# Matmul stages of a decoder layer: one work pool of aligned tiles, weights combined ahead of the resident rows, and shared in the attention output

## The chip, the cores and the metric

The kernel runs on one core of a Trainium2 chip. The metric is the device time of one execution in microseconds (us); lower is better. The engines of the core are TensorE (PE, matmuls), VectorE (DVE), ScalarE (ACT), GpSimd (POOL) and SyncE (SP, which here issues the DMA transfers). Each works through its own instructions in order and waits for others by semaphores.

## The reference

One layer with two parallel branches, on x of 2048 x 1024 in float32:

```python
shift, scale, gate = split(silu(c) @ w_ada + b_ada, 3)
h = x * (1 + scale) + shift
q, k, v, g_attn, u, b_gate, c_gate, g_conv, m_attn, m_conv = split(h @ w_in)
# o: three dilated causal sliding-window attention groups, merged by their softmax sums
a_out = (o * silu(g_attn)) @ w_attn_out
z = c_gate * u                          # zp: z behind two zero rows
y_conv = cw[0] * zp[:-2] + cw[1] * zp[1:-1] + cw[2] * zp[2:] + conv_b
s_out = (b_gate * y_conv * silu(g_conv)) @ w_conv_out
merged = sigmoid(m_attn) * a_out + sigmoid(m_conv) * s_out
y = merged @ w_o
out = layer_norm(2 ** 0.25 * x + (1 + gate) * y) * ln_g + ln_b
```

## The kernel before

Each float32 operand is split into a high and a low part, and a product is three matmuls (high x high, high x low, low x high; lines L681 to L683). Part 1, up to about 1202 us, makes scale and shift, the attention's projections, the attention and its merge; the merge's last work on DVE runs on to 1239 us. The change doesn't touch it.

The last stage (from L596 on) computes all other products as Strassen-Winograd products of 2 x 2 blocks, seven instead of eight. Two kinds of operands go into these:

- T, the resident side: `t_row` makes, from two wide tiles (`big`) with one row of blocks each, the seven combinations of row i, split into th and tl (11 operations on DVE, the rest on ACT). Four rows of T stay on the chip for a whole stage.
- S, the streamed weights: `stationary_parts` loads two blocks (`raw`), forms the combinations (`xs`, `s4`, in place in `raw`) and splits them into w2h, w2l, w1h and w1l (eight operations on DVE). Each step has its own S.

A step's `products` are 7 products x 4 rows x 3 = 84 matmuls of 128x512, in the order 1, 2, 6, 5, 7, 4, 3. ACT copies three intermediate sums out of PSUM (`t` tiles, L687), and a consumer takes the results on DVE. `step` loads and forms S, runs the products of the step before (`flush`) and puts its own on the list `todo`; so S is one step ahead of its products. At the start of a stage `flush` comes first, then T's rows, and then the first step's S.

The stages in order, each but the second with a pool of its own (`workspace(number of big, number of t)`):

1. Projections and their consumers, pool (4, 8): for p = 0, 1 (halves of the sequence) four rows of T and 24 steps (conv and gates alternating, then eight mixes). p = 1 starts within the same pool.
2. Attention output, pool (7, 8): for p = 0, 1 two rows of T (of om_scr) and four steps of half size (S of 128x512), each with two big tiles of sigmoid values loaded from sg_scr and stored to pa_scr. During p = 0 `gate_part` makes the gate from w_ada on DVE (L236).
3. Conv output, pool (6, 8): for p = 0, 1 four rows of T (of y_scr) and four steps; each loads two tiles of sg_scr and two of pa_scr, POOL adds the two (L890), and mg_scr is stored.
4. w_o and layer norm ("norm stage"), pool (5, 6): the rows of T are those of w_o, times the gate (L916); then eight steps with S made of mg_scr, and the norm on DVE, ACT and POOL (L927 to L944), two result tiles a step.

The order of the work on each engine is set when the program is built: a scheduler orders what the code writes by estimated times; tiles of a pool are used in turn, and a new use waits until the old one is done.

Of the kernel before, what the change touches and what calls it, by code (L numbers as in the profile page):

```python
# [11 lines left out]
F32 = mybir.dt.float32  # L12
F32R = mybir.dt.float32r
AF = mybir.ActivationFunctionType
# [40 lines left out]
def layer_kernel(ctx: ExitStack, tc: tile.TileContext, x, xm, xn, cvec, wada, bada, w_main, w_v,  # L55
# [548 lines left out]
    def big():  # L604
        return work[0].tile([P, PAIR + 2], F32, name="big", bufs=work[1])

    def half(name="t"):
        return work[0].tile([P, CH], F32, name="t", bufs=work[2])

    @contextmanager  # L610
    def workspace(n_big, n_half):
        with tc.tile_pool(name="work", bufs=1, reuse_waits="tile") as w:
            work[:] = [w, n_big, n_half]
            yield w
# [30 lines left out]
    def stationary_parts(w, raw1, raw2, n):  # L645
# [21 lines left out]
        s4 = w.tile([P, n], F32, name="s4")  # L667
# [47 lines left out]
    def step(w, src1, src2, n, T, rows, consumer):  # L715
        raws = []
        for s in ((src1, src2) if src2 is not None else (src1,)):
            raw = w.tile([P, DM], F32, name="raw", bufs=3)
            SP.dma_start(raw, s)
# [13 lines left out]
    gate_acc = const.tile([P, 4], F32, name="gate_acc")  # L733

    with workspace(4, 8) as w:
        for n in range(KT):
            SP.dma_start(cw[:, n, :3], convw[n])
        SP.dma_start(cw[:, :, 3], convb)
        for p in range(2):
            T = {}  # L740
            flush()
            for i in range(4):
                xa, xb = big(), big()
                for t, k in ((xa, i), (xb, i + 4)):
                    for cc in range(2):
                        SP.dma_start(t[:, cc * CH:(cc + 1) * CH], xn[2 * p + cc, :, k, :])
                    S.activation(t[:, :PAIR], t[:, :PAIR], AF.Identity, scale=scp[:, k:k + 1],
                                 bias=mod[:, 0, k:k + 1])
                t_row(T, i, xa, xb)
            for n in range(KT):  # L750
                box = {}

                def conv(box=box, n=n):
                    z = box["z"] = big()
                    V.tensor_copy(z[:, 0:2], halo[:, n, :])

                    def zmul(at):
                        def f(r, bank):
                            t = half()
                            V.tensor_add(t, r, bank)  # L760
                            V.tensor_mul(z[:, 2 + at:2 + at + CH], t, z[:, 2 + at:2 + at + CH])
                        return f

                    def u1(r, bank):
                        V.tensor_add(z[:, 2 + CH:], r, bank)
                        V.tensor_mul(z[:, 2 + CH:], z[:, 2 + CH:], box["c1"])
                        V.tensor_copy(halo[:, n, :], z[:, PAIR:])
                        y = box["y"] = big()[:, :PAIR]
                        S.activation(y, z[:, 0:PAIR], AF.Identity, scale=cw[:, n, 0:1], bias=cw[:, n, 3:4])
                        V.scalar_tensor_tensor(y, z[:, 1:PAIR + 1], cw[:, n, 1:2], y, op0=ALU.mult, op1=ALU.add)  # L770
                        V.scalar_tensor_tensor(y, z[:, 2:PAIR + 2], cw[:, n, 2:3], y, op0=ALU.mult, op1=ALU.add)

                    def c1(r, bank):
                        box["c1"] = half()
                        V.tensor_add(box["c1"], r, bank)

                    return sum_to(z[:, 2:2 + CH]), u1, zmul(0), c1

                def gates(box=box, n=n, p=p):
                    g = big()[:, :PAIR]  # L780
                    y = box["y"]

                    def g1(r, bank):
                        V.tensor_add(g[:, CH:], r, bank)
                        V.tensor_mul(y, y, g)
                        S.activation(g, g, AF.Sigmoid)
                        V.tensor_mul(y, y, g)
                        V.tensor_mul(y, y, box["b"])
                        SP.dma_start(y_scr[p, n], y)

                    def bs(at):
                        def f(r, bank):
                            V.tensor_add(box["b"][:, at:at + CH], r, bank)
                        return f

                    box["b"] = big()[:, :PAIR]
                    return sum_to(g[:, :CH]), g1, bs(0), bs(CH)

                step(w, w_main[W_U + n], w_main[W_C + n], CH, T, range(4), conv)
                step(w, w_main[W_GC + n], w_main[W_B + n], CH, T, range(4), gates)  # L800
            for d in range(KT):
                def mixes(p=p, d=d):
                    m = [big()[:, :PAIR] for _ in range(2)]

                    def out_(k):
                        S.activation(m[k], m[k], AF.Sigmoid)
                        SP.dma_start(sg_scr[p, k, d], m[k])

                    def c12(r, bank):
                        V.tensor_add(m[0][:, CH:], r, bank)  # L810
                        out_(0)

                    def c21(r, bank):
                        V.tensor_add(m[1][:, :CH], r, bank)
                        out_(1)

                    return sum_to(m[0][:, :CH]), c12, c21, sum_to(m[1][:, CH:])

                step(w, w_main[W_MA + d], w_main[W_MC + d], CH, T, range(4), mixes)
        flush()  # L820


    with workspace(7, 8) as w:
        cbox = []

        def gate_part(k):
            if k == 0:
                cbox.append(w.tile([P, DM], F32, name="cb"))
                silu_c(cbox[0], big()[:, :DM])
            wt = w.tile([P, DM], F32, name="raw", bufs=3)  # L830
            SP.dma_start(wt, wada[2, k])
            dot_v(wt, cbox[0], half()[:, :256], gate_acc)
            dot_end(2, k, gate_acc)
            V.tensor_scalar_add(mod[:, 2, k:k + 1], mod[:, 2, k:k + 1], 1.0)

        for p in range(2):
            T = {}
            rows = range(2 * p, 2 * p + 2)
            for i in range(2):
                xa, xb = big(), big()  # L840
                for t, j in ((xa, i), (xb, i + 2)):
                    for cc in range(2):
                        SP.dma_start(t[:, cc * CH:(cc + 1) * CH], om_scr[2 * p + cc, :, j, :])
                t_row(T, 2 * p + i, xa, xb)
            for d in range(0, KT, 2):
                def part(p=p, d=d):
                    m = [big()[:, :PAIR] for _ in range(2)]
                    for k in range(2):
                        SP.dma_start(m[k], sg_scr[p, 0, d + k])

                    def gated(k, at):
                        def f(r, bank):
                            t = half()
                            V.tensor_add(t, r, bank)
                            V.tensor_mul(m[k][:, at:at + CH], m[k][:, at:at + CH], t)
                            if (k, at) in ((0, CH), (1, 0)):
                                SP.dma_start(pa_scr[p, d + k], m[k])
                        return f

                    return gated(0, 0), gated(0, CH), gated(1, 0), gated(1, CH)  # L860
# [5 lines left out]
        flush()  # L866

    with workspace(6, 8) as w:
        for p in range(2):
            T = {}  # L870
            flush()
            for i in range(4):
                xa, xb = big(), big()
                for t, k in ((xa, i), (xb, i + 4)):
                    SP.dma_start(t[:, :PAIR], y_scr[p, k])
                t_row(T, i, xa, xb)
            for d in range(0, KT, 2):
                def merged(p=p, d=d):
                    m = [big()[:, :PAIR] for _ in range(2)]
                    a_ = [big()[:, :PAIR] for _ in range(2)]  # L880
                    for k in range(2):
                        SP.dma_start(m[k], sg_scr[p, 1, d + k])
                        SP.dma_start(a_[k], pa_scr[p, d + k])
# [129 lines left out]
```

## Time and profile before

| | |
|---|---|
| runs | 2795.53, 2800.72, 2800.15 us; median 2800.15 |
| profiled execution | 2793.6 us, its span 2791.8 us |
| mean granted clock of TensorE | 0.958 |
| PE busy | 2519.3 us, 90% of the span |
| DVE busy | 1696.2 us, 61% |
| ACT busy | 1012.5 us, 36% |
| POOL busy | 158.4 us, 6% |
| DMA | 333.34 MB, mean 119 GB/s |

The share of an engine is a mean over all stages. What a stage is limited by is read from the stretches (busy time of each engine, granted clock, DMA) and from the waits of the engine that should never stand still, PE. A granted clock of 1.00 is the level of 2.4 GHz, 0.5 that of 1.2 GHz; a stretch's number is a mean of both. "Idle before" is the time an engine waited ahead of an instruction, and the name behind the arrow what released it.

### The profile page before, as it was taken

How to read it: one execution, taken by the hardware profiler on the slowest of the kernel's cores; microseconds unless marked ns; L12 is line 12 of the kernel's file. 1: busy time of each engine (PE TensorE's matmuls, PEld its weight loads, DVE VectorE, ACT ScalarE, POOL GpSimd, SP SyncE). 2: the span in 40 equal slices, each digit the busy share in tenths (PEclk: the TensorE clock that was granted, in tenths of full speed). 3: DMA queues.
4: the chain of work that ended last, by engine and by line, in shares of the span. 5: the costliest groups of instructions: out<-in, count | busy, mean ns of one | idle time of the engine just before them, and what ended most of it. 6: DMA issues, size and time to landing. Idle time of an engine off the chain costs nothing. (4 is left out here: it accounts for less than half of the span.)

```text
span 2791.8 us, 31786 instructions
## 1 busy us (share of the span) xinstructions
PE 2519.3 (90%) x12070; PEld 2115.6 (76%) x12070; DVE 1696.2 (61%) x2816; ACT 1012.5 (36%) x1691; POOL 158.4 (6%) x126
## 2 busy tenths in 40 slices
PE   6999999999999999927999999899999966787597
PEld 4898999989887888816888888688888744666475
DVE  8335333243346675658666654876664388886997
ACT  4234333233333443324333343533333334342432
POOL 2000000000000000000000000000000000213144
PEclk9999999999999999968999999999999978899799
DMA  7224233232334363442122233321222276555342
GB/s 254 78 87 125 82 95 104 66 116 91 104 100 148 120 204 103 133 150 77 61 68 76 68 113 115 112 68 61 68 81 101 78 268 217 200 201 192 125 173 92
DMA packets 156270, 333.34 MB, mean 119 GB/s; under 512 B 18279, under 2 KB 69555, under 8 KB 156116
## 3 DMA queue, kind: packets, MB, share of 16 engines
q1 hardware_dynamic: 156116, 331.31, 35.9%
q8 instruction: 94, 1.54, 0.2%
q14 instruction: 60, 0.49, 0.1%
HBM read 268.03 MB, written 63.23 MB: 119 GB/s over the span
## 5 line engine op out<-in xcount | busy, mean ns | idle before, releaser
L681 PE MATMUL pb<-th,w2h 128*128 128x512 f32 x1632 | 653.3, 402 | 144.7 <-ACT w2h L102 122.7
L683 PE MATMUL pb<-th,w2l 128*128 128x512 f32 x1632 | 648.0, 399 | 55.9 <-DVE w2l L103 55.9
L682 PE MATMUL pb<-tl,w2h 128*128 128x512 f32 x1632 | 650.9, 400 | 2.5 <-DVE tl L103 2.5
L681 PEld LDWEIGHTS pb<-th,w2h 128*128 128x128 f32 x1632 | 312.1, 191 | 229.2 <-ACT w2h L102 127.3
L103 DVE TENSOR_TENSOR wlo<-raw,whi 128x1024 fp32r<-128x1024 f32 x155 | 189.6, 1223 | 419.8 <-ACT whi L102 412.9
L683 PEld LDWEIGHTS pb<-th,w2l 128*128 128x128 f32 x1632 | 312.0, 191 | 132.6 <-DVE w2l L103 59.9
L682 PEld LDWEIGHTS pb<-tl,w2h 128*128 128x128 f32 x1632 | 312.5, 192 | 76.7 <-DVE tl L103 4.3
L140 PE MATMUL mm<-hhi,whi 128*128 128x512 f32 x856 | 341.9, 399 | 22.0 <-ACT hhi L102 22.0
L142 PE MATMUL mm<-hhi,wlo 128*128 128x512 f32 x856 | 335.9, 392 | 3.1 <-DVE wlo L103 3.1
L141 PE MATMUL mm<-hlo,whi 128*128 128x512 f32 x856 | 335.5, 392 | 1.7 <-DVE hlo L103 1.7
L102 ACT CAST whi<-raw 128x1024 fp32r<-128x1024 f32 x155 | 162.6, 1049 | 443.1 <-issue 183.7
L186 PE MATMUL mm<-whi,hhi 128*128 128x256 f32 x768 | 246.1, 322 | 3.7 <-ACT hhi L102 3.7
L188 PE MATMUL mm<-whi,hlo 128*128 128x256 f32 x768 | 244.9, 323 | 3.3 <-DVE hlo L103 3.1
L187 PE MATMUL mm<-wlo,hhi 128*128 128x256 f32 x768 | 244.6, 321 | 1.1 <-DVE wlo L103 1.1
L103 DVE TENSOR_TENSOR w2l<-raw,w2h 128x1024 fp32r<-128x1024 f32 (+1 forms) x144 | 168.3, 1169 | 118.7 <-ACT w2h L102 118.5
L102 ACT CAST w2h<-raw 128x1024 fp32r<-128x1024 f32 (+1 forms) x144 | 144.1, 1001 | 238.4 <-PE pb L682 209.5
L687 ACT COPY t<-pb 128x512 f32<-128x512 f32 x216 | 125.7, 583 | 271.1 <-PE pb L683 269.2
L140 PEld LDWEIGHTS mm<-hhi,whi 128*128 128x128 f32 x856 | 161.9, 189 | 54.5 <-ACT hhi L102 24.0
L142 PEld LDWEIGHTS mm<-hhi,wlo 128*128 128x128 f32 x856 | 161.5, 189 | 38.3 <-DVE wlo L103 4.2
L186 PEld LDWEIGHTS mm<-whi,hhi 128*128 128x128 f32 x768 | 181.9, 237 | 8.2 <-ACT hhi L102 6.6
L141 PEld LDWEIGHTS mm<-hlo,whi 128*128 128x128 f32 x856 | 161.9, 189 | 33.6 <-DVE hlo L103 2.9
L188 PEld LDWEIGHTS mm<-whi,hlo 128*128 128x128 f32 x768 | 181.1, 237 | 6.2 <-DVE hlo L103 5.5
(197 smaller groups left out, 3545.6 us busy)
## 6 DMA issues: line engine op xcount, KB each, us to landing
raw<-in_w_main SPq DMA_DIRECT2D x208, 512.0 KB
raw<-in_w_v SPq DMA_DIRECT2D x48, 512.0 KB
sg_scr<-big SPq DMA_DIRECT2D x32, 512.0 KB
big<-sg_scr SPq DMA_DIRECT2D x32, 512.0 KB
ab<-al_scr SPq DMA_DIRECT2D x48, 256.0 KB
wt<-in_wada SPq DMA_DIRECT2D x16, 512.0 KB
xs<-in_xm SPq DMA_DIRECT2D x32, 256.0 KB
o_scr<-o SPq DMA_DIRECT2D x32, 256.0 KB
```

What stands on the lines that cost most here:

```text
L102: S.copy(hi, src)
L103: V.tensor_sub(lo, src, hi.bitcast(F32))
L140: PE.matmul(ps, hi[:, sl], xh, start=k == 0, stop=False)
L141: PE.matmul(ps, hi[:, sl], xl, start=False, stop=False)
L142: PE.matmul(ps, lo[:, sl], xh, start=False, stop=k == n - 1)
L186: PE.matmul(o, a[0], b[0], start=start, stop=False)
L187: PE.matmul(o, a[0], b[1], start=False, stop=False)
L188: PE.matmul(o, a[1], b[0], start=False, stop=stop)
L681: PE.matmul(bank, hi[:, sl], th, start=first, stop=False, **kw)
L682: PE.matmul(bank, hi[:, sl], tl, start=False, stop=False, **kw)
L683: PE.matmul(bank, lo[:, sl], th, start=False, stop=n == len(rows) - 1, **kw)
L687: S.copy(r, bank)
```

## The change

One pool serves the whole last stage: 4 big tiles, 2 rows, 7 small tiles (`t`). A big tile has 1088 floats instead of 1026. `step` takes `uses`, a list of (T, rows, consumer), and `pre`, which makes T's rows; it forms S, flushes the step before, runs `pre`, and puts the products of all uses on the list. The attention output makes T's rows of both halves first, and each S (four instead of eight) serves both. `gate_part` goes to the mixes of p = 0. The conv output takes pa_scr, and the norm stage x, in halves through small tiles; the norm's scaled addition of x is done in halves.

```diff
     def big():
-        return work[0].tile([P, PAIR + 2], F32, name="big", bufs=work[1])
+        return work[0].tile([P, PAIR + 64], F32, name="big", bufs=work[1])
+    def row():
+        return work[0].tile([P, DM], F32, name="row", bufs=2)
...
-        s4 = w.tile([P, n], F32, name="s4")
+        s4 = half()[:, :n]
...
-    def step(w, src1, src2, n, T, rows, consumer):
+    def load_parts(w, src1, src2, n):
         raws = []
...
-        S_ = stationary_parts(w, raws[0], raws[1], n)
+        return stationary_parts(w, raws[0], raws[1], n)
+
+    def step(w, src1, src2, n, uses, pre=None):
+        S_ = load_parts(w, src1, src2, n)
         flush()
-        todo.append(lambda: products(S_, T, rows, *consumer()))
+        if pre is not None:
+            pre()
+        for T, rows, consumer in uses:
+            todo.append(lambda T=T, rows=rows, consumer=consumer: products(S_, T, rows, *consumer()))
...
-    with workspace(4, 8) as w:
+    w = ctx.enter_context(tc.tile_pool(name="work", bufs=1, reuse_waits="tile"))
+    work[:] = [w, 4, 7]
+    def t_rows(T, loads):
+        def pre():
+            for i, load in loads:
+                xa, xb = big(), big()
+                load(xa, xb)
+                t_row(T, i, xa, xb)
+        return pre
...
-            flush()
-            for i in range(4):
-                xa, xb = big(), big()
...
+        pre = t_rows(T, [(i, load_h(i)) for i in range(4)])
...
+            step(w, w_main[W_U + n], w_main[W_C + n], CH, [(T, range(4), conv)], pre)
+            pre = None
...
+                if p == 0:
+                    gate_part(d)
...
-    with workspace(7, 8) as w:
-        for p in range(2):
...
-                if p == 0:
-                    gate_part(d)
-                    gate_part(d + 1)
-                step(w, w_ao[d // 2], None, 256, T, rows, part)
-        flush()
+    pre = t_rows(T, [(2 * p + i, load_o(p, i)) for p in range(2) for i in range(2)])
...
+        step(w, w_ao[d // 2], None, 256, [(T, range(2 * p, 2 * p + 2), part(p)) for p in range(2)], pre)
...
-    with workspace(6, 8) as w:
...
-                    a_ = [big()[:, :PAIR] for _ in range(2)]
...
+                        a_, t = half(), half()
+                        SP.dma_start(a_, pa_scr[p, d + k, :, at:at + CH])
...
-    with workspace(5, 6) as w:
-        gate_row = w.tile([P, DM], F32, name="row")
...
-                xr = [big()[:, :DM] for _ in range(2)]
-                for k in range(2):
-                    SP.dma_start(xr[k], x[(tb + k) * P:(tb + k + 1) * P, :])
...
-                    V.scalar_tensor_tensor(z, xr[k], ALPHA, z, op0=ALU.mult, op1=ALU.add)
...
+                    xr = half()
+                    SP.dma_start(xr, x[rows, hs])
+                    V.tensor_add(z[:, hs], r, bank)
+                    V.scalar_tensor_tensor(z[:, hs], xr, ALPHA, z[:, hs], op0=ALU.mult, op1=ALU.add)
```

In an order's row stand the line, the operation, and output<-inputs with the numbers of the tiles. First DVE behind the attention, before: the last operations of T (tl) and then S of the first step (w2l, xs, s4, w1l).

```order
L103 TENSOR_TENSOR tl73_10751<-big_10720,th73_10750 128x512
L103 TENSOR_TENSOR tl33_10760<-big_10721,th33_10759 128x512
L103 TENSOR_TENSOR tl43_10756<-t_10730,th43_10755 128x512
L103 TENSOR_TENSOR w2l_10768<-raw_10763,w2h_10767 128x1024
L659 TENSOR_TENSOR xs_10771<-xs_10771,raw_10763 128x512
L663 TENSOR_TENSOR raw_10765<-raw_10763,raw_10765 128x512
L668 TENSOR_TENSOR s4_10783<-raw_10763,xs_10771 128x512
L103 TENSOR_TENSOR w2l_10775<-xs_10771,w2h_10774 128x1024
L103 TENSOR_TENSOR w2l_10780<-raw_10765,w2h_10779 128x1024
L103 TENSOR_TENSOR w1l_10786<-s4_10783,w1h_10785 128x512
```

After, from the last operation of the merge on (its helpers' line numbers are 3 lower; s4 is now a t):

```order
L576 TENSOR_TENSOR o03_10428<-o03_10428,gt3_10486 128x512
L103 TENSOR_TENSOR w2l_10596<-raw_10591,w2h_10595 128x1024
L655 TENSOR_TENSOR xs_10599<-raw_10593 128x512
L656 TENSOR_TENSOR xs_10599<-xs_10599,raw_10591 128x512
L660 TENSOR_TENSOR raw_10593<-raw_10591,raw_10593 128x512
L665 TENSOR_TENSOR t_10611<-raw_10591,xs_10599 128x512
L625 TENSOR_TENSOR t_10625<-big_10617 128x512
L103 TENSOR_TENSOR w2l_10603<-xs_10599,w2h_10602 128x1024
L103 TENSOR_TENSOR w2l_10608<-raw_10593,w2h_10607 128x1024
L103 TENSOR_TENSOR w1l_10614<-t_10611,w1h_10613 128x512
L626 TENSOR_TENSOR t_10626<-big_10618,t_10625 128x512
L103 TENSOR_TENSOR tl10_10629<-big_10617,th10_10628 128x512
```

S of the first step has moved ahead of nearly all of T; the first row's differences (t<-big) mix with it.

Then PE at the start of the conv output, before (thpi and tlpi are product p of row i; pb is a bank of PSUM):

```order
L681 MATMUL pb_18496<-th10_18287,w2h_18440 128x512
L682 MATMUL pb_18496<-tl10_18288,w2h_18440 128x512
L681 MATMUL pb_18511<-th20_18291,w2h_18440 128x512
L682 MATMUL pb_18511<-tl20_18292,w2h_18440 128x512
L683 MATMUL pb_18496<-th10_18287,w2l_18441 128x512
L681 MATMUL pb_18496<-th11_18326,w2h_18440 128x512
L682 MATMUL pb_18496<-tl11_18327,w2h_18440 128x512
L683 MATMUL pb_18496<-th11_18326,w2l_18441 128x512
L681 MATMUL pb_18496<-th12_18365,w2h_18440 128x512
```

After:

```order
L678 MATMUL pb_18388<-th10_18209,w2h_18040 128x512
L678 MATMUL pb_18403<-th20_18213,w2h_18040 128x512
L679 MATMUL pb_18388<-tl10_18210,w2h_18040 128x512
L680 MATMUL pb_18388<-th10_18209,w2l_18041 128x512
L679 MATMUL pb_18403<-tl20_18214,w2h_18040 128x512
L680 MATMUL pb_18403<-th20_18213,w2l_18041 128x512
L678 MATMUL pb_18436<-th50_18223,w2h_18047 128x512
L679 MATMUL pb_18436<-tl50_18224,w2h_18047 128x512
L680 MATMUL pb_18436<-th50_18223,w2l_18048 128x512
L678 MATMUL pb_18388<-th11_18248,w2h_18040 128x512
L678 MATMUL pb_18469<-th40_18233,w2h_18052 128x512
L678 MATMUL pb_18538<-th10_18209,w2h_18362 128x512
```

Before, the first matmul that needs w2l (L683) is the fifth, and all others stand behind it in the order of the products; w2l itself is made behind T. After, products 1, 2, 5 and 4 of row 0 come first and then mix with the next row and with the next step's product 1 (pb_18538).

Last SP in the middle of the norm stage, before: x comes in whole tiles, both ahead of the stores of the step before it.

```order
L927 DMA big_20481<-in_x 128x1024
L927 DMA big_20482<-in_x 128x1024
L719 DMA raw_20613<-mg_scr_89 128x1024
L944 DMA out_y<-big_20322 128x1024
L944 DMA out_y<-big_20321 128x1024
L719 DMA raw_20769<-mg_scr_89 128x1024
L927 DMA big_20639<-in_x 128x1024
```

After, in halves (t<-in_x):

```order
L969 DMA out_y<-big_20258 128x1024
L952 DMA t_20542<-in_x 128x512
L969 DMA out_y<-big_20257 128x1024
L969 DMA out_y<-big_20422 128x1024
L716 DMA raw_20725<-mg_scr_89 128x1024
L952 DMA t_20615<-in_x 128x512
L969 DMA out_y<-big_20421 128x1024
L716 DMA raw_20887<-mg_scr_89 128x1024
L952 DMA t_20660<-in_x 128x512
```

A half tile of x for one step now stands behind the stores (out_y) of the step before.

## Rows read from the trace of the kernel before

**Rows 1.** Waits of PE: line, awaited operation, us in total, times, longest.
```profile
PE pb L681 <- ACT w2h L102: 122.7, 9, 54.6
PE pb L683 <- DVE w2l L103: 55.9, 5, 24.9
```

**Rows 2.** Stretches of the last stage: busy us per engine, PEclk, DMA share, GB/s.
```profile
1201.90:1315.00 113.10, 41.85 (x169) 33.39 (x170) 83.46 (x126) 44.71 (x62) 0.00 (x0) 0.68 0.41 130
1315.00:1744.40 429.40, 429.40 (x1849) 348.01 (x1847) 265.88 (x329) 152.81 (x185) 0.00 (x0) 1.00 0.24 84
1744.40:1797.40 53.00, 45.01 (x170) 33.16 (x170) 46.49 (x71) 35.81 (x51) 0.00 (x0) 0.94 0.36 120
2226.80:2355.50 128.70, 90.65 (x337) 66.93 (x336) 108.54 (x260) 48.28 (x86) 0.00 (x0) 0.83 0.65 233
2355.50:2430.30 74.80, 41.77 (x170) 33.45 (x170) 60.69 (x88) 30.95 (x47) 10.12 (x7) 0.77 0.62 218
2430.30:2473.90 43.60, 40.55 (x169) 32.50 (x168) 26.21 (x34) 12.73 (x17) 14.62 (x8) 0.96 0.58 193
2473.90:2526.20 52.30, 43.57 (x170) 32.08 (x170) 48.86 (x69) 24.86 (x39) 12.28 (x7) 0.93 0.59 199
2564.70:2653.30 88.60, 43.59 (x177) 34.19 (x176) 74.48 (x103) 34.99 (x50) 10.58 (x6) 0.73 0.45 151
2653.30:2775.80 122.50, 119.18 (x505) 93.95 (x503) 105.11 (x147) 42.13 (x50) 50.97 (x24) 1.00 0.39 140
```

**Rows 3.** Timeline of DVE: start, us, line, output; [idle before <-releaser]. First stretch.
```profile
1246.19 0.69 DVE L628 TENSOR_TENSOR t<-big 128x512 f32<-128x512 f32 x1 [7.34 <-ACT big L747]
...
1273.35 0.68 DVE L103 TENSOR_TENSOR tl<-t,th 128x512 fp32r<-128x512 f32 x1
1273.95 1.22 DVE L103 TENSOR_TENSOR w2l<-raw,w2h 128x1024 fp32r<-128x1024 f32 x1
...
1279.77 1.22 DVE L103 TENSOR_TENSOR w2l<-raw,w2h 128x1024 fp32r<-128x1024 f32 x1
```

**Rows 4.** Timeline of DVE, p=1 of the projections.
```profile
1774.65 0.69 DVE L103 TENSOR_TENSOR tl<-big,th 128x512 fp32r<-128x512 f32 x1
```

**Rows 5.** Timeline of DVE, p=1 of the conv output.
```profile
2504.50 0.68 DVE L103 TENSOR_TENSOR tl<-t,th 128x512 fp32r<-128x512 f32 x1
```

**Rows 6.** Timeline of DVE, attention output.
```profile
2235.25 0.69 DVE L103 TENSOR_TENSOR tl<-big,th 128x512 fp32r<-128x512 f32 x1 [7.55 <-ACT th L102]
```

**Rows 7.** Groups of DVE operations in the attention output.
```profile
L236 DVE CUSTOM_DVE_ANT_0 t<-raw,cb 128x256 f32<-128x256 f32 x32 | 13.3, 416 | 0.9 <-DMA raw<-in_wada 0.8
L103 DVE TENSOR_TENSOR w2l<-raw,w2h 128x512 fp32r<-128x512 f32 x16 | 11.0, 685 | 1.3 <-ACT w2h L102 1.2
```

**Rows 8.** Timeline of DVE, conv output, p=0.
```profile
2356.59 0.69 DVE L855 TENSOR_TENSOR big<-big,t 128x512 f32<-128x512 f32 x1
2363.40 0.69 DVE L628 TENSOR_TENSOR t<-big 128x512 f32<-128x512 f32 x1 [6.12 <-DMA big<-y_scr]
...
2390.60 0.68 DVE L103 TENSOR_TENSOR tl<-t,th 128x512 fp32r<-128x512 f32 x1
```

**Rows 9.** Timeline of DVE, start of the norm stage.
```profile
2575.44 1.23 DVE L916 TENSOR_TENSOR big<-big,row 128x1024 f32<-128x1024 f32 x1 [9.12 <-DMA big<-in_w_o]
...
2610.71 0.68 DVE L103 TENSOR_TENSOR tl<-t,th 128x512 fp32r<-128x512 f32 x1
```

**Rows 10.** Groups of operations on DVE, then POOL, six steps of the norm stage.
```profile
L931 DVE SCALAR_TENSOR_TENSOR big<-big 128x1024 f32<-128x1024 f32 x12 | 19.0, 1582 | 0.2
...
L658 DVE TENSOR_TENSOR xs<-raw 128x512 f32<-128x512 f32 x4 | 11.1, 2779 | 0.0
...
L940 DVE SCALAR_TENSOR_TENSOR rs<-mv,rs 128x1 f32<-128x1 f32 x12 | 1.9, 159 | 9.6 <-POOL rs L939 9.6
...
L943 POOL TENSOR_TENSOR big<-big,row 128x1024 f32<-128x1024 f32 x12 | 38.0, 3166 | 36.0 <-DVE big L942 16.9 <-issue 16.2 <-DVE mv L937 2.9
```

**Rows 11.** Groups of DVE operations in 22 steps of the projections.
```profile
L658 DVE TENSOR_TENSOR xs<-raw 128x512 f32<-128x512 f32 x22 | 15.2, 692 | 0.8
```

More of the change, by code (lines that the diff above doesn't have):

```diff
@@ L1 @@
 import math
-from contextlib import ExitStack, contextmanager
+from contextlib import ExitStack
 import numpy as np
@@ L748, in layer_kernel @@
                                  bias=mod[:, 0, k:k + 1])
[L749 to L819, printed above, removed]
@@ new lines, in layer_kernel, with mixes, out_, c12 @@
+        for d in range(KT):
+            def mixes(p=p, d=d):
+                m = [big()[:, :PAIR] for _ in range(2)]
+                def out_(k):
+                    S.activation(m[k], m[k], AF.Sigmoid)
+                    SP.dma_start(sg_scr[p, k, d], m[k])
+                def c12(r, bank):
+                    V.tensor_add(m[0][:, CH:], r, bank)
+                    out_(0)
+                def c21(r, bank):
+                    V.tensor_add(m[1][:, :CH], r, bank)
+                    out_(1)
@@ L862, in layer_kernel @@
                 if p == 0:
                     gate_part(d)
-                    gate_part(d + 1)
-                step(w, w_ao[d // 2], None, 256, T, rows, part)
-        flush()
-    with workspace(6, 8) as w:
[L869 to L873, printed above, removed]
+                return sum_to(m[0][:, :CH]), c12, c21, sum_to(m[1][:, CH:])
+            step(w, w_main[W_MA + d], w_main[W_MC + d], CH, [(T, range(4), mixes)])
@@ new lines, in layer_kernel, with load_o, load, part @@
+    T = {}
+    def load_o(p, i):
+        def load(xa, xb):
+            for t, j in ((xa, i), (xb, i + 2)):
+                for cc in range(2):
+                    SP.dma_start(t[:, cc * CH:(cc + 1) * CH], om_scr[2 * p + cc, :, j, :])
+        return load
+    pre = t_rows(T, [(2 * p + i, load_o(p, i)) for p in range(2) for i in range(2)])
+    for d in range(0, KT, 2):
+        def part(p, d=d):
+            def consumer():
+                m = [big()[:, :PAIR] for _ in range(2)]
+                for k in range(2):
+                    SP.dma_start(m[k], sg_scr[p, 0, d + k])
+                def gated(k, at):
+                    def f(r, bank):
+                        t = half()
+                        V.tensor_add(t, r, bank)
+                        V.tensor_mul(m[k][:, at:at + CH], m[k][:, at:at + CH], t)
+                        if (k, at) in ((0, CH), (1, 0)):
+                            SP.dma_start(pa_scr[p, d + k], m[k])
+                    return f
+                return gated(0, 0), gated(0, CH), gated(1, 0), gated(1, CH)
+            return consumer
+        step(w, w_ao[d // 2], None, 256, [(T, range(2 * p, 2 * p + 2), part(p)) for p in range(2)], pre)
+        pre = None
@@ L899, in layer_kernel @@
[L899 to L912 removed]
+            return load
@@ L913, in layer_kernel, with load_w, load @@
+    T, rows_ = {}, {}
+    def load_w(i):
+        def load(xa, xb):
+            if i == 0:
+                gate_row = rows_["gate"] = row()
+                for hh in range(2):
+                    pg = ps_bank()
+                    for k in range(4):
+                        PE.transpose(pg[:, k * P:(k + 1) * P],
+                                     mod[:, 2, hh * 4 + k:hh * 4 + k + 1].to_broadcast([P, P]), ident)
+                    S.copy(gate_row[:, hh * CH:(hh + 1) * CH], pg)
             for t, k in ((xa, i), (xb, i + 4)):
```

208 lines of the change are left out of this document (110 added, 98 removed).

## Prediction

> **What bounds the kernel now.** I read the list of waits first, then the stretches, then the timelines of VectorE (DVE) around each place where TensorE (PE) stands still. E is the moment at which a stage's last matmul ends; the bounds of the stretches are such ends of steps (84 matmuls each, so two steps show some 169).
>
> From 1201.9 us on, PE's idle time has in the main one cause: it waits for S, the combinations of the weights. 122.7 us go to the high part that ScalarE writes and 55.9 us to the low part that DVE writes [rows 1]. In 22 undisturbed steps PE is busy all the time and a step takes 429.4/22 = 19.5 us, 0.232 us a matmul, at a granted clock of 1.00, the level of 2.4 GHz [rows 2]. Against that the first two steps of a stage, 39.0 us undisturbed, take far longer: 113.1 us behind the attention (part of it merges that stay), 74.8 us in the conv output, 88.6 us in the norm stage; the attention output takes 128.7 us for 336 matmuls, 78 us undisturbed. All these lie at a mean clock of 0.68 to 0.83, so in part at the level of 1.2 GHz after PE stood still [rows 2]. Two places have the same resident rows T to make and lose only 14.0 and 13.3 us: p=1 of the projections (53.0) and p=1 of the conv output (52.3) [rows 2]. There no pool opens, S is made before T, and the products of two steps mix as each row of T comes. The other four open a new pool and make T first, S behind it.
>
> These two places are my measure. From the end of DVE's last T operation to the end of the second step it took 1797.4 - 1775.3 = 22.1 us in one [rows 2, 4] and 2526.2 - 2505.1 = 21.1 us in the other [rows 2, 5]. The program order of the changed kernel has all four other boundaries in that form, so I ask when T's last operation ends and add 21.5.
>
> **Behind the attention.** Now T's rows run from 1246.2 to 1273.95, 27.8 us for four rows, 0.6 us an operation (11 a row on DVE), and S follows, 5.8 us from 1273.95 to the start of its last operation and 0.6 for the one made earlier: 6.4 [rows 3]. In the new order S goes ahead, so T ends about 6.4 us later, 1281 with a little waiting; plus 22.1 this is 1303 against 1315.0: **-12** (-8 if the raw weights, now issued ahead of the rows of x, delay these; -14 if S fits in DVE's 7.34 us of idle time ahead of row 0 [rows 3]).
>
> **Projections, p=1:** the same form before and after, 0. The gate's products move in among p=0's mixes. They cost 32 x 0.416 = 13.3 us of DVE [rows 7] and, with reductions, about 1.9 us for each of 8 steps. DVE is busy 265.88 of 429.4 us in such steps [rows 2], 7.4 us idle in each: hidden. If it weren't, 8 x 1.9 = 15 us. Their weight takes a third "raw" slot per step, and the next step's raw load waits for it, a step ahead of need.
>
> **Attention output.** Four of eight S (half width: three operations at 0.6, five at 0.34, 3.5 us each) and all gate products leave DVE, 14 + 15 us of its 108.54 [rows 2, 7]; four 512 KB loads go too. T's four rows come at the start. Row 0 can be made during the last mixes; row 1 needs tiles that the last mixes store, and starts when row 0 does now, E + 8.4 [rows 6]. Three rows at 6.6 us end at E + 28. By the new order 48 matmuls stand ahead of the first that needs the last row, and 288 x 0.232 = 67 remain: E + 95 against 128.7: **-33** (-26 to -37). Eight groups of products at 9.7 us have four big tiles, two groups' worth, where seven stood: a tile is stored and loaded again within one group's time, which is tight.
>
> **Conv output, p=0.** The same with y: its first load now ends DVE's idle time at 2363.40, 7.9 us behind E = 2355.5 [rows 8]. Row 0 will be earlier, rows 1 to 3 run from E + 7.9 to E + 27.7, a few parts of S among them; plus 21.5 this is E + 49 against 74.8: **-25** (-15 to -29). **p=1:** rows end as now, since four tiles instead of six make row 1 wait for a store: 0 (3 either way). The steps between lose 43.6 - 39.0 = 4.6 us now [rows 2]; the half loads and S made earlier give some back: **-2** (-5 to +2). The halves of the attention's part are read by POOL alone, so a late one holds POOL's addition and the store behind it, not DVE.
>
> **Norm stage.** Here T's rows are longer, 2 x 1.2 us for the multiplication by the gate on top: 9.0 us. They run now from 2575.4 (9.12 us of idle time for the load ahead) to 2611.3, E + 46.6 [rows 9]. The gate's row is made from eight transposes behind E in both kernels, but w_o is loaded by then: rows from E + 2 to E + 37, and S (6.4, and 3 of the next step's) is already made. For PE alone that would be -30. But this stage belongs to DVE: 122.5/6 = 20.4 us a step where PE wants 19.5, with PE at full clock [rows 2], so only what DVE gains counts: 9.5 us of the rows' delay and 9.3 of S, -18.8. Against it, x comes in halves through the seven small tiles. A half waits for a tile that the step before frees, and SyncE (SP) issues it behind the store of the result, so behind GpSimd's (POOL's) addition. DVE works in order: behind its waiting x operation stand the statistics of this step and S of the next, and PE waits for these. Following the new order row by row I find 0 to 1.5 us a step and take 0.6: 8 x 0.6 = +4.8. Together **-14** (-30 if DVE's margin is larger than it looks, +10 with 3.6 us a step). The tail is the same.
>
> In this stage 4 of DVE's xs operations take 2779 ns [rows 10], elsewhere 692 [rows 11]: they stand behind the multiplication that starts POOL's 3166 ns addition [rows 10]. The Trainium skill, "SBUF — State Buffer", section "Who interferes with whom", says that a DVE instruction with two SBUF inputs and a GpSimd instruction that reads SBUF exclude each other, the first to issue keeping the ports to its end. The rows agree. By that rule alone the split changes nothing in the sum unless other two-input operations land behind an addition, which is the second rival.
>
> **Sum:** -12 - 33 - 25 - 2 - 14 = -86. The profiled execution took 2793.6 us, so 2707.6; the median of the runs is 6.6 above it (2800.15), so the forecast is **2714 us**. The terms' ends don't come together; taken as independent they give 28 us up and 18 down (roots of the sums of squares): own range 2696 to 2742. What runs of this kernel can tell from no change is 0.2%, 5.6 us.
>
> **Rivals.**
> First, that the change doesn't do what it says: S still comes late at the four boundaries, since the raw loads stand in SP's queue behind stores, or the slots of raw are held. Then only work removed from the attention output counts, where DVE is busy 84% of the time [rows 2]: -29, 2771 us. For it: SP works in order, and in DVE's order S does wait for its load. Against: in the two measured places S was ready by this same order, and the new rows of SP issue raw a step early. Chance 0.09.
>
> Second, the norm stage loses to POOL. If every one of the additions blocks DVE for its whole length, 38.0 us in six steps, less the 4 x 2.09 = 8.3 us that xs now loses [rows 10, 11], that is 4.9 us a step, 40 us in eight: the norm term goes from -14 to +21, and the time to 2749 us. For it: four half operations instead of two whole ones stand in the way, two for each result. Against: DVE already waits 9.6 us in the six steps for POOL's power operation [rows 10], time that the blocks can take the place of. Chance 0.13.
>
> Third, slower: four big tiles. If each of the 8 groups of the attention output and the 8 steps of the conv output waits for its tiles in series, store then load, at the 6.1 us that such a chain shows on DVE [rows 8], this is 16 x 6.1 = 98 us against 86 gained: 2812 us. It decides from 86/16 = 5.4 us a group on. For it: the tiles go from 7 and 6 to 4, and the attention output moves 233 GB/s already, DMA engines 65% busy [rows 2]. Against: a step of the conv output has 19.5 us to hide the chain in, and x and the attention's part no longer use big tiles. Chance 0.05.
>
> **How the numbers follow.** Forecast 0.73, first rival 0.09, second 0.13, third 0.05. The range 2680 to 2758 reaches down nearly to the point where all lower ends come together (-118 us, 2682), since the norm's term alone could give more, and up past the second rival. Faster by over 0.2%: 0.94, all but the third and parts of it; within 0.2%: 0.02, the third at its point of balance; slower: 0.04.
>
> **What would show it.** Right: PE's waits for S from 1200 us on fall from 179 us [rows 1] to under 40 and turn into shorter waits for T; the attention output takes about 95 us, the first two steps of the conv output about 50, of the norm stage under 75; the norm's later steps 20 to 22 us. Wrong: PE or DVE waiting for sg_scr or pa_scr loads in every group (third rival); xs or the half operations at over 2 us, or waits of DVE for in_x (second); waits for S still over 100 us (first).

## The result and the profile after

The changed kernel takes 2727.64 us (median; 2724.08 to 2729.01), the one before 2797.84 us (with a fourth run beside the three listed above): a ratio of 0.9747, 95% interval 0.973 to 0.9764. The forecast was 2714 us with a range of 2680 to 2758. The profiled executions went from 2793.6 to 2724.08 us. So the direction and the range held, and 70 us came where 86 were forecast; but the parts of these 70 are not those of the forecast.

The stretches of the changed kernel, cut at the same ends of steps as [rows 2] (columns as there: start:end, length, busy us of PE, weight loads, DVE, ACT and POOL, granted clock, DMA share, GB/s):

```profile
1201.90:1306.20 104.30, 48.67 (x169) 34.16 (x170) 79.95 (x123) 43.00 (x60) 0.00 (x0) 0.71 0.46 143
1306.20:1725.20 419.00, 419.00 (x1849) 346.68 (x1847) 281.51 (x422) 155.34 (x188) 0.00 (x0) 1.00 0.28 96
1725.20:1780.00 54.80, 44.62 (x169) 32.53 (x169) 45.06 (x70) 35.11 (x50) 0.00 (x0) 0.94 0.31 107
1780.00:2199.00 419.00, 419.00 (x1849) 346.87 (x1848) 265.06 (x337) 153.44 (x188) 0.00 (x0) 1.00 0.25 86
2199.00:2305.30 106.30, 90.66 (x338) 65.06 (x337) 83.24 (x138) 39.76 (x70) 0.00 (x0) 0.89 0.63 223
2305.30:2357.10 51.80, 45.40 (x169) 31.77 (x168) 44.23 (x68) 23.38 (x38) 6.25 (x5) 0.93 0.54 184
2357.10:2401.70 44.60, 39.32 (x169) 31.08 (x169) 34.32 (x42) 14.60 (x21) 14.18 (x10) 1.00 0.75 255
2401.70:2455.80 54.10, 44.22 (x170) 31.99 (x169) 46.02 (x67) 22.45 (x37) 9.15 (x7) 0.94 0.54 179
2455.80:2501.10 45.30, 39.37 (x170) 31.02 (x169) 34.73 (x41) 12.93 (x19) 13.81 (x10) 1.00 0.77 255
2501.10:2564.10 63.00, 49.60 (x178) 35.68 (x177) 58.89 (x84) 27.70 (x43) 4.66 (x4) 0.84 0.40 130
2564.10:2704.30 140.20, 122.89 (x505) 98.03 (x503) 115.75 (x169) 44.88 (x53) 46.16 (x27) 0.94 0.40 133
```

Two stretches of before that [rows 2] leaves out, the other 22 steps of the projections and the last two of the conv output:

```profile
1797.40:2226.80 429.40, 429.40 (x1849) 348.00 (x1847) 258.65 (x323) 148.74 (x182) 0.00 (x0) 1.00 0.22 75
2526.20:2564.70 38.50, 38.50 (x169) 31.38 (x168) 22.87 (x29) 6.77 (x10) 14.80 (x10) 1.00 0.55 180
```

| stretch | before | after | change | forecast |
|---|---|---|---|---|
| behind the attention, two steps | 113.1 | 104.3 | -8.8 | -12 |
| projections, 44 undisturbed steps | 858.8 | 838.0 | -20.8 | none |
| projections, p=1, two steps | 53.0 | 54.8 | +1.8 | 0 |
| attention output | 128.7 | 106.3 | -22.4 | -33 |
| conv output p=0, two steps | 74.8 | 51.8 | -23.0 | -25 |
| conv output, two steps between | 43.6 | 44.6 | +1.0 | -2 |
| conv output p=1, two steps | 52.3 | 54.1 | +1.8 | 0 |
| conv output, last two steps | 38.5 | 45.3 | +6.8 | 0 |
| norm stage, two steps | 88.6 | 63.0 | -25.6 | |
| norm stage, six steps | 122.5 | 140.2 | +17.7 | |
| tail | 16.0 | 18.0 | +2.0 | -14 for the three rows of the norm stage |

The sum is -69.5, the difference of the spans. Two rows stand out: a gain of 20.8 us in steps that the forecast took as untouched, and 17.7 us given back in the norm stage right behind a gain of 25.6. The three rows of the norm stage are best read together, -5.9: the cut at PE's steps divides DVE's work differently in the two kernels (12 of the 16 additions on POOL fall into the six steps before, 14 after).

PE's waits from 1200 us on (line and awaited operation, us in total, times, longest), against [rows 1]:

```profile
PE pb L678 <- ACT th L102: 91.3, 34, 50.3
PE pb L678 <- DVE t L905: 11.2, 6, 2.5
PE pb L679 <- DVE tl L103: 10.9, 19, 2.3
PE pb L678 <- ACT t L684: 10.6, 4, 6.4
PE pb L678 <- DVE big L953: 8.4, 4, 4.2
PE pb L678 <- ACT w2h L102: 3.4, 7, 0.5
...
PE pb L680 <- DVE w2l L103: 1.0, 2, 0.5
```

The 178.6 us of waits for w2h and w2l have become 4.4; waits for T (th, tl) took their place, 50.3 of them the one behind the attention, and new ones for the consumers (t, big). All of PE's waits from there on together fall from 210.1 to 139.6 us.

### The profile page after: what moved, and what is told of

Read it like the earlier page. It is cut to its first block, busy times and chain, and to the rows that moved or that the text cites. A ratio compares the mean times of both kernels' runs of the same rounds, so it can differ in the third digit from the quotient of the medians.

```text
span 2722.3 us, 31895 instructions
## 1 busy us (share of the span) xinstructions
PE 2518.6 (93%) x12070; PEld 2114.6 (78%) x12070; DVE 1684.8 (62%) x2800; ACT 1002.0 (37%) x1675; POOL 142.3 (5%) x126
## 4 chain that ended last, share of the span: by engine, by line
PE 72%; DVE 12%; DMA 8%; issue 4%; ACT 2%; POOL 1%; SPq 0%; POOLq 0%; DVEq 0%; ACTq 0%
PE pb L678 12%; PE pb L679 12%; PE pb L680 12%; PE mm L140 6%; PE mm L141 6%; PE mm L142 6%; PE mm L188 4%; PE mm L186 4%; PE mm L187 4%; DVE tl L103 2%; DMA og<-o_scr 1%; PE pt L367 1%; DVE w2l L103 1%; DMA xs<-in_xn 1%; DVE hlo L103 1%
## 5 line engine op out<-in xcount | busy, mean ns | idle before, releaser
L680 PE MATMUL pb<-th,w2l 128*128 128x512 f32 x1632 | 640.4, 396 | 1.0 <-DVE w2l L103 1.0
L102 ACT CAST w2h<-raw 128x1024 fp32r<-128x1024 f32 (+1 forms) x136 | 139.6, 1027 | 275.0 <-PE pb L679 262.0
```

The source lines that it names most:

```text
L102: S.copy(hi, src)
L680: PE.matmul(bank, lo[:, sl], th, start=False, stop=n == len(rows) - 1, **kw)
```

## Experiments

Part 1 is not equally long in each execution: PE's last matmul of it ends at 1197.7 to 1208.9 us (at 1201.8 in both profiles above). So stretches are compared below, the first one from the end of that matmul; whole times are compared by their ratios to before, measured on the same chip, and a difference of two ratios is given in us of before's 2797.84.

**The faster steps.** One matmul after another in an undisturbed step, first before, then after (start, duration):

```profile
1400.03 0.40 PE L681 MATMUL pb<-th,w2h 128*128 128x512 f32 x1
1400.27 0.40 PE L682 MATMUL pb<-tl,w2h 128*128 128x512 f32 x1
1400.50 0.39 PE L683 MATMUL pb<-th,w2l 128*128 128x512 f32 x1
1400.73 0.39 PE L681 MATMUL pb<-th,w2h 128*128 128x512 f32 x1
```

```profile
1401.53 0.39 PE L678 MATMUL pb<-th,w2h 128*128 128x512 f32 x1
1401.75 0.39 PE L679 MATMUL pb<-tl,w2h 128*128 128x512 f32 x1
1401.98 0.39 PE L680 MATMUL pb<-th,w2l 128*128 128x512 f32 x1
1402.21 0.39 PE L678 MATMUL pb<-th,w2h 128*128 128x512 f32 x1
```

Both are at a clock of 1.00 without a wait. Between 1400 and 1700 us two starts lie 232.4 ns apart on average before, between 228 and 241, and 226.7 after, always 226 or 227. By the addresses in the two programs, T's tiles start at 96 modulo 256 bytes in both; the weights' tiles w2h, w2l, w1h and w1l at 224 in the projections of before, behind four big tiles of 4128 bytes each, and at 96 after, since the single pool has them ahead of the big tiles. Four runs test this. The first adds one tile to before's first pool. That moves every tile of the pool by 128 bytes, not only the weights' as its expectation has it; of these a matmul reads only the weights'.

```diff
     with workspace(4, 8) as w:
+        w.tile([P, 32], F32, name="pad")
```

> The kernel before, with 128 bytes left free at the start of the projections' pool, so that the weights' tiles (w2h, w2l, w1h, w1l) lie at the same address modulo 256 as T's tiles (96; before 224); nothing else moves and no other stage changes. Theory (place of the weights): a matmul of the projections starts every 226.7 ns as in the changed kernel, instead of 232.4; 44 steps x 84 x 5.7 ns = 21 us less, about 2777 us. Rival (it is the width and place of the big tiles, or the changed order of loads): the steps stay at 19.5 us and the time at that of before.

Measured: 2777.55 us, ratio 0.9908 (0.9891 to 0.9924). The 22 steps of p=0:

```profile
1320.80:1739.70 418.90, 418.90 (x1849) 346.66 (x1847) 265.59 (x329) 152.70 (x184) 0.00 (x0) 1.00 0.25 86
```

429.4 us became 418.9, twice: 21.0 us by 128 free bytes. The second run does the reverse to the changed kernel, with the same tile at the start of its pool.

> The changed kernel, with 128 bytes left free at the start of its pool, so that the weights' tiles lie at 224 modulo 256 and T's at 96, as in the projections of before. Theory (place of the weights): the projections' steps go from 19.05 back to 19.5 us, 21 us more in 44 steps, and some 3 to 5 us in the later stages, about 2750 us. Rival (big tiles, or the new order): the steps stay at 19.05 us and the time near 2728.

Measured: 2756.45 us, ratio 0.9839 (0.9825 to 0.9854), and the 22 steps are back at the old length:

```profile
1308.30:1737.80 429.50, 429.50 (x1849) 347.94 (x1847) 281.53 (x422) 155.41 (x188) 0.00 (x0) 1.00 0.28 94
```

The third run sets the width of a big tile back (`PAIR + 64` to `PAIR + 2`).

> The changed kernel with big tiles of 1026 floats as before; the weights' tiles stay where they are, since the big tiles lie behind them. Theory (place of the weights): a step of the projections stays at 19.05 us, and the time within 0.2% of the changed kernel's. Rival (the big tiles' alignment is what the matmuls gain from): 19.5 us a step, 21 us more; DVE's operations on big tiles would then be longer too.

```profile
1306.00:1725.10 419.10, 419.10 (x1849) 346.58 (x1847) 281.40 (x422) 155.44 (x188) 0.00 (x0) 1.00 0.28 96
```

2723.72 us in its one run, 419.1 us for the steps: the width that the change sets is not what gains; its order of the tiles in the pool is. The last one leaves 128 bytes free ahead of T (`tp.tile([P, 32], F32, name="pad")`), so that all tiles move.

> The changed kernel with 128 bytes left free ahead of T's tiles, so that T's and the weights' tiles both lie at 224 modulo 256 (both at 96 in the changed kernel). Theory (what counts is that both lie alike): a projections' step stays at 19.05 us. Rival (the weights' own address modulo 256 counts, 96 is good and 224 bad): 19.5 us, 21 us more in 44 steps.

```profile
1313.00:1732.10 419.10, 419.10 (x1849) 346.69 (x1847) 281.56 (x422) 155.57 (x188) 0.00 (x0) 1.00 0.28 96
```

The steps keep 19.05 us (2732.19 us in one run, in which part 1 ended 5.4 us later). So a difference of 128 bytes between the places of the two operands costs 5.7 ns a matmul, and the weights' own place does not. Why the engine minds is not settled by this, and "modulo 256" is no more than the measure used here: T's tiles follow each other at 2048 bytes and the weights' slices of 128 columns at 512, so these runs can't tell 256 from 512.

**The boundaries: S ahead, or one pool.** The next run puts the first step's S behind T again, in the four stages where it was there before:

```diff
-        S_ = load_parts(w, src1, src2, n)
+        if pre is None or not late[0]:
+            S_ = load_parts(w, src1, src2, n)
         flush()
         if pre is not None:
             pre()
+            if late[0]:
+                S_ = load_parts(w, src1, src2, n)
```

> The changed kernel, but at the four boundaries where S was late before (behind the attention, attention output, conv output p=0, norm stage) the first step's S is formed behind T's rows again. Theory (S ahead of T, so that the products of two steps mix with T's rows): the four boundaries give back most of what they gained: 9 + 23 + 10 to 22 + 15 to 25 us, 50 to 75 us in all, 2780 to 2800 us. Rival (one pool without boundaries, loads that start earlier): only S's own 6.4 us (3.5 in the attention output) is late, about 23 us, 2750 us.

Measured: 2745.27 us, ratio 0.9797 (0.9782 to 0.9811), by the ratios 14 us above the changed kernel: far from the theory's 50 to 75, and less than the rival's 23. Behind the attention the whole gain goes back: from part 1's last matmul to the end of the second step it takes 112.6 us (104.6 after, 113.3 before; 104.0 to 106.0 in the other kernels with S ahead). The conv output's first two steps take 57.6 us (51.8 after, 74.8 before), those of the norm stage 69.7 (63.0, 88.6); the attention output loses nothing (104.8; 106.3). PE's waits for S are back only in part, and 54.3 us of the first row is the one behind the attention:

```profile
PE pb L678 <- ACT w2h L102: 60.9, 7, 54.3
PE pb L678 <- ACT th L102: 35.4, 26, 5.4
PE pb L680 <- DVE w2l L103: 17.2, 2, 16.7
```

Next, the order stays but each stage opens a pool of its own size again:

```diff
+    def new_pool():
+        flush()
+        pools.close()
+        pool = pools.enter_context(tc.tile_pool(name="work", bufs=1, reuse_waits="tile"))
+        work[:] = [pool, 4, 7]
+        return pool
...
+    w = new_pool()
```

> The changed kernel, but with a pool of its own (same sizes: 4 big, 2 rows, 7 small) for the projections, the attention output, the conv output and the norm stage, each opened when the one before has ended; the order of S ahead of T inside a stage stays, and the places of the weights too. Theory (one pool lets the next stage's first loads, S and first row of T go ahead of the last products of the stage before): the three boundaries give back 10 to 15 us each, 30 to 45 us in all, 2758 to 2775 us. Rival (the order S, T inside a stage and the shared S of the attention output are what gained): within 10 us of the changed kernel, under 2738 us.

Measured: 2756.61 us, ratio 0.986 (0.9843 to 0.9878), 32 us given back, within the theory's range: the first two steps take 71.7 us in the conv output and 80.6 in the norm stage, the attention output 111.9. That is 43 us at the three boundaries; the last two steps of the conv output (40.3 us) and the six of the norm stage (135.1) are 5 us shorter each. SP's own timeline of this run around E = 2307.6 shows it (issue, time taken or waited, transfer):

```profile
2300.10 9.71 SPq L885 DMA_DIRECT2D pa_scr<-big  x3
2309.86 1.27 SPq L716 DMA_DIRECT2D raw<-in_w_co  x2
2311.17 2.42 SPq L901 DMA_DIRECT2D big<-y_scr  x4
```

The weights and y are asked for only behind the last store of the stage before, and PE's first matmul waits:

```profile
2318.49 0.79 PE L678 MATMUL pb<-th,w2h 128*128 128x512 f32 x1 [10.69 <-ACT th L102]
```

In the changed kernel the same y loads begin 6.4 us ahead of the stage's end at 2305.3, between the stores:

```profile
2298.89 0.32 SPq L891 DMA_DIRECT2D big<-y_scr  x1
2300.41 0.33 SPq L716 DMA_DIRECT2D raw<-in_w_co  x1
2301.21 0.32 SPq L891 DMA_DIRECT2D big<-y_scr  x1
2305.53 2.16 SPq L876 DMA_DIRECT2D pa_scr<-big  x2
```

In this run `new_pool` also calls `flush` ahead of S. That isn't what holds the loads: in the run before, with one pool and S behind `flush`, y and the weights were asked for at 2311.89 and 2314.20, ahead of that stage's end at 2316.6. So both halves of the reading count: behind the attention S's place alone, at the conv output and the norm stage the pool's boundary (20 and 18 us) more than S's place (6 and 7).

**The attention output.** This run gives each half its own S again (eight instead of four) and puts the gate's products back:

```diff
-        step(w, w_ao[d // 2], None, 256, [(T, range(2 * p, 2 * p + 2), part(p)) for p in range(2)], pre)
-        pre = None
+        for p in range(2):
+            step(w, w_ao[d // 2], None, 256, [(T, range(2 * p, 2 * p + 2), part(p))], pre)
+            pre = None
...
+                if p == 0:
+                    gate_part(d)
+                    gate_part(d + 1)
```

> The changed kernel with the attention output's work as before: each half makes its own S (eight instead of four, eight loads), and the gate's products stand in it again instead of in the mixes; T's rows of both halves still come first and the pool is one. Theory (DVE bounds the attention output, so what left it counts): 14 + 15 us more on a DVE that is busy 83 of 106 us; the stage goes from 106 to 118 to 125 us, about 2743 us. Rival (T's rows, loads and PE bound it, the removed work was hidden): under 5 us more.

```profile
2204.40:2333.90 129.50, 99.10 (x337) 67.23 (x336) 112.64 (x258) 50.00 (x88) 0.00 (x0) 0.83 0.64 231
```

2767.76 us, ratio 0.9879 (0.9855 to 0.9903), 37 us above the changed kernel where 15 were expected. The stage takes 129.5 us, as long as before, with DVE busy 112.64 of them; after, 83.24 of 106.3. So without the removed work the stage gains nothing, and it is worth 23 us there; the run doesn't divide this between the shared S and the gate's products. It is not enough by itself either, as 5.6 us went back with a pool of its own. That the conv output and the norm stage up to its last matmul are also 23 us longer here (421.9 us against 399.0) is not explained.

**What the conv output and the norm stage gave back.** Two guesses first, both on the halves that go through small tiles. In one, POOL issues the conv output's halves (`G.dma_start(a_, ...)`):

> The changed kernel, but the conv output's loads of the attention's part (halves of pa_scr) are issued by POOL instead of SP. Theory (a half's load waits in SP's queue for a small tile, and the weights' loads behind it come late, so DVE and PE stand still): the conv output's steps 54, 55, 58 and 59, now 21.7, 22.9, 21.4 and 23.9 us, come down to 19.1 to 20, 8 to 12 us less in all, about 2718 us. Rival (DVE's own work and POOL's port set these steps): no change, 2728 us.

2721.47 us, ratio 0.9731 (0.9716 to 0.9745), whose interval overlaps that of the changed kernel. The last two steps of the conv output take 41.2 us instead of 45.3, those between 45.3 instead of 44.6. DVE's waits for the weights of the conv output did not go, 17.8 us against 8.9 in the six steps behind the first two: the explanation by SP's queue falls. Nor is the shorter end shown to come from the queue: in the versions of the changed kernel that leave these loads to SP the last two steps take 40.3 to 50.3 us, 40.3 in the run with pools of their own. In the other, no x is loaded, and ln_b's row is added in its place:

> The changed kernel without the load of x: the norm stage adds ln_b's row, which is on the chip, in its place (x's residual is left out). All DVE and POOL operations stay. Theory (the halves of x wait for small tiles and for SP, and hold DVE): the steps of 24.6, 28.1 and 27.6 us go; the norm stage from 2564 on loses 10 to 18 us, about 2713 us. Rival (DVE's work and POOL's additions bound the stage): within 4 us of the changed kernel.

2723.11 us, ratio 0.9737 (0.9722 to 0.9751); the norm stage's eight steps take 201.5 us (203.2): the rival's answer, the halves of x are not the cause. Neither is the number of small tiles (`work[:] = [w, 4, 8]`):

> The changed kernel with 8 small tiles instead of 7. Theory (the number of small tiles holds the copies out of PSUM and the halves' loads in conv output and norm stage): 4 to 10 us less, about 2720 us. Rival (their number doesn't matter): within 3 us of the changed kernel.

2727.81 us, ratio 0.9758 (0.9737 to 0.978). That leads to POOL. DVE's groups in the six steps of the changed kernel, and POOL's:

```profile
L954 DVE SCALAR_TENSOR_TENSOR big<-t,big 128x512 f32<-128x512 f32 x26 | 22.0, 851 | 3.7 <-DMA t<-in_x 3.6
...
L103 DVE TENSOR_TENSOR w2l<-raw,w2h 128x1024 fp32r<-128x1024 f32 x10 | 16.5, 1653 | 3.2 <-ACT w2h L102 3.2
...
L655 DVE TENSOR_TENSOR xs<-raw 128x512 f32<-128x512 f32 x5 | 6.3, 1256 | 1.0 <-DMA raw<-mg_scr 1.0
```

```profile
L968 POOL TENSOR_TENSOR big<-big,row 128x1024 f32<-128x1024 f32 x14 | 36.7, 2620 | 42.8 <-DVE big L967 38.4 <-DVE mv L961 4.4
```

Against 692 ns for xs in the projections [rows 11] these are long. Before, the delay fell on xs and on five of the twelve scaled additions (2.1 us instead of 1.2; 1582 ns in the mean [rows 10]); now it falls on several operations. One case, POOL's addition and DVE's operations from then on:

```profile
2658.71 2.72 POOL L968 TENSOR_TENSOR big<-big,row 128x1024 f32<-128x1024 f32 x1 [3.75 <-DVE big L967]
2659.15 3.36 DVE L103 TENSOR_TENSOR w2l<-raw,w2h 128x1024 fp32r<-128x1024 f32 x1
2662.43 0.67 DVE L953 TENSOR_TENSOR big<-t,pb 128x512 f32<-128x512 f32 x1
```

w2l starts 0.44 us behind POOL's addition and ends 1.08 us behind its end. The next run leaves POOL's addition out:

```diff
-                    G.tensor_add(z, z, rows_["b"])
```

> The changed kernel without the addition of ln_b on POOL (the bias of the norm is left out); POOL keeps only the power operation there. Theory (POOL's additions hold DVE's operations with two inputs, and DVE bounds the norm stage): the two-input operations return to 0.69 and 1.22 us, and the stage from the end of the conv output, now 203 us to its last matmul, loses 12 to 20 us, about 2712 us. Rival (DVE's own work, in order, behind T's rows): under 4 us less.

2707.26 us, ratio 0.9657 (0.964 to 0.9675): by the ratios 25 us below the changed kernel. The six steps take 123.0 us instead of 140.2 and the tail 12.2 instead of 18.0. DVE is busy 99.06 us of the six steps instead of 115.75, so nearly all of their 17.2 us are the lengths of its operations, which are undisturbed:

```profile
L954 DVE SCALAR_TENSOR_TENSOR big<-t,big 128x512 f32<-128x512 f32 x26 | 17.4, 674 | 3.5 <-DMA t<-in_x 3.5
...
L103 DVE TENSOR_TENSOR w2l<-raw,w2h 128x1024 fp32r<-128x1024 f32 x10 | 12.2, 1222 | 6.5 <-ACT w2h L102 6.5
```

This prices POOL's additions in the changed kernel; it doesn't say that the change brought that price. No run leaves them out of the kernel before, but its trace shows the same delay: summed over DVE's operations of the whole norm stage that take longer than their undisturbed 0.69 or 1.22 us, some 18 us before and some 20 after (an estimate from the two traces). Both stages as a whole, first before, then after:

```profile
2564.70:2791.80 227.10, 162.98 (x681) 128.14 (x679) 188.62 (x262) 79.60 (x102) 67.31 (x34) 0.87 0.40 139
2501.10:2722.30 221.20, 172.60 (x681) 133.71 (x679) 185.12 (x268) 75.06 (x98) 56.90 (x35) 0.88 0.38 126
```

DVE's busy time falls by 3.5 us and its idle time by 2.4. The price itself points to a version with the whole computation: ln_b added on DVE itself, and POOL's queue for the conv output's halves.

```diff
-                        SP.dma_start(a_, pa_scr[p, d + k, :, at:at + CH])
+                        G.dma_start(a_, pa_scr[p, d + k, :, at:at + CH])
...
-                    G.tensor_add(z, z, rows_["b"])
+                    V.tensor_add(z, z, rows_["b"])
```

> The changed kernel with the whole computation, but ln_b is added on DVE instead of POOL, and the conv output's halves are loaded through POOL's queue as in the run with that queue. Theory (an addition on POOL costs DVE up to 3 us where DVE itself needs 1.2): of the 20 us that leaving the addition out gave, 16 x 1.2 = 19 us of DVE's work come back, but only where DVE has no idle time (it is busy 99 of 123 us there), so 12 to 17 us are kept, and 4 to 6 us from the queue: 2706 to 2712 us. Rival (DVE is the bound of the norm stage whatever POOL does): the 19 us come back in full, 2722 us.

```profile
2573.50:2700.60 127.10, 118.40 (x505) 92.84 (x503) 114.26 (x185) 45.15 (x53) 13.06 (x13) 1.00 0.43 143
```

2714.79 us, ratio 0.9671 (0.9658 to 0.9684), below both kernels: 127.1 us for the six steps, with DVE doing 14 additions more at 1219 ns each and still busy 1.5 us less than in the changed kernel. Its idle time falls from 24.5 to 12.8 us, of it the waits for POOL's power operation from 10.4 to 4.4. By the ratios the version keeps about 21 of the 25 us, as much as forecast from the changed kernel's 2727.64 (2706 to 2712), though its median on its chip lies higher, as that of before does (2805.68). How much of it is the queue's is not shown.

## Why the prediction was right, and where it was not

- The reading of the bound was right: PE waited for S at four boundaries, and these waits went from 178.6 to 4.4 us. As said beforehand they turned into waits for T, but not into short ones only: PE's waits of all kinds still add up to 139.6 us. The gate's products are hidden in the mixes, as forecast: the 22 steps of p = 0, which have them, take 419.0 us like those of p = 1.
- The step "each boundary costs T's last operation plus 21.5 us" held for the conv output, where T's last operation starts at 2335.31 and the second step ends at 2357.1 (51.8 us against 49 to 50 forecast). Behind the attention T ended when forecast, at 1280.4 against 1281, but the rest took 25.9 us instead of 22.1: -8.8 instead of -12. The step put S's place and the pool's boundary into one number; by the runs S's place is worth 14 us and the common pool 32.
- The term of the attention output was too large: 106.3 us against 95. T's last row operation (2230.35) ended 32.0 us behind E = 2199.0 instead of 28. By then 48 matmuls had started, as forecast, but the other 288 took 74 us instead of 67. The forecast took them at the undisturbed pace; here PE waited 4.8 us more, and the mean clock was 0.98. Its other half, that the work taken off DVE counts, is shown by the run that puts it back.
- The norm stage's term was mis-sized, -5.9 against -14. Of DVE's time the forecast let 9.5 us of waiting and 9.3 of S go, and charged 4.8 for x in halves: 4.7 us less of idle time and 9.3 less of busy time. Measured are 2.4 and 3.5. The halves of x are not it: the run without them is 1.7 us shorter there. POOL's additions hold DVE, the second rival's mechanism, but nearly as much before: the forecast saw it on xs alone and missed it on the scaled additions, so this adds some 2 us to the stage (18 before, 20 after) and not 40. What keeps the rest is open. As the Trainium skill, "SBUF — State Buffer", section "Who interferes with whom", has it, who issues first keeps the ports to the end of the instruction; the runs agree, with w2l at 1653 ns beside POOL's additions and 1222 without, and in the case shown above w2l, issued second, ended only behind POOL's addition.
- What failed outright is a cost at nothing: the projections' undisturbed steps. The forecast has no term for the places of the tiles and never asked why matmuls of one shape started 228 to 241 ns apart. 20.8 of the 69.5 us come from there. That is luck: everything else together gained 48.7 us where the terms say 86, and by this alone the time would have been about 2748 us, still inside the stated range but outside the 2696 to 2742 of the sum.
- Of the signs, the waits for S and the first two steps of the conv output and the norm stage came; the attention output (106.3 against about 95 us) and the norm's later steps (23.4 us each against 20 to 22) did not.
- The last two steps of the conv output lost 6.8 us that no term had. POOL's additions and the weights' late loads both show there; which it is stays open.
- The third rival (four big tiles in series) did not come: PE has no long wait for sg_scr or pa_scr.

## What to carry to other kernels

Matmuls of one shape that start at uneven distances without a wait are a cost to look for: compare the places of both operands in memory, and move one. In this kernel a boundary between pools was a wait for the last store of the stage before, even with S ahead of T. Where DVE bounds a stage, work given to POOL can cost DVE more than it takes off: compare the lengths of DVE's operations there with those of a stage without POOL, and do it in the kernel before as well, since a cost found only after the change need not come from it.

## What the runs showed that was not expected

- Matmuls 128x512 in float32 halves: 226.7 ns from start to start where both operands' tiles lie alike modulo 256 bytes (both at 96, both at 224), 232.4 ns where they differ by 128, at a granted clock of 1.00 in both. Modulo 512 would fit these runs as well.
- Additions of 128x1024 on POOL, 2.6 to 3.2 us each in the mean, are slower for the whole than those on DVE of 1.22 us, even on a DVE that is busy 114.26 of 127.1 us: it was busy 115.75 us of the same six steps while POOL did them.
